# A 31-tap depthwise convolution traced tap by tap among the projections

## The chip, the cores and the metric

The kernel runs on one core of a Trainium2 chip. The metric is the device time of one launch in microseconds. The engines that matter here are TensorE (PE in the rows), VectorE (DVE), ScalarE (ACT) and GpSimd (POOL); the queue of SyncE (SP) issues most transfers. Each engine works through its own list of instructions in order and waits on semaphores for the others.

## The reference

One program computes a chain of layers on a sequence of 1024 tokens of width 1024. The change lies in the fourth stage of it, the even layer. Its core:

```python
hn = rmsnorm(x, norm_w)
proj = hn @ w_in
z_a, xbc, dt_raw, glu_v, glu_g, z_b = jnp.split(proj, idx, axis=-1)
xbc = silu(causal_dwconv(xbc, conv_w, conv_b))        # 4 taps
xs, bs, cs = jnp.split(xbc, ...)
dt = softplus(dt_raw + dt_bias)
y = ssd_chunked(xs, dt, a, bs, cs, d_skip)            # state-space scan
y_a = rmsnorm(y * silu(z_a))                          # per group
u = glu_v * sigmoid(glu_g)
u = causal_dwconv(u, dw_w, dw_b)                      # 31 taps, 1024 channels
u = silu(layernorm(u, ln_w, ln_b))
return x + concat([y_a, u * silu(z_b)]) @ w_out
```

The convolution of 31 taps works on each channel by itself: y[c, t] is the bias plus the sum over k of w[k, c] * u[c, t - 30 + k].

## The kernel before

`even` runs from about 1480 to 2125 us of the span. Matrix products are made in three matmuls each, from a high and a low half of both operands: `mm3` issues high x high (L264), high x low (L265) and low x high (L266) for every block of 128 rows. Weights come in by `load_w`: a transfer into `wr_t`, ScalarE makes the high half `wh_t` (L198), and VectorE (two thirds) and GpSimd (one third) make the low half `wl_t` (L203). The first L266 of a weight therefore waits for an L203 of VectorE.

The layer goes through four groups g = 0 to 3. A group holds, in the order in which it is traced:

- the gate z of the group (L1401), 192 matmuls of 256 columns, each bank read by VectorE (L1405);
- `glu(2g+1)`: 96 matmuls, then VectorE writes the channel block `u_t` (L1360) and hands it to `conv31`;
- `xbc` four times, for B, C, x0 and x1: 48 matmuls each, then on VectorE three short taps (L1380) and a product (L1383);
- in group 0 alone the running sums `cs` and their transposed copy `csT` (L1448), which the mask matmuls of every group read (L1488);
- transposes of B, x0 and x1 (L1437 for x0 and x1, after their L1383), mask matmuls (L1488, L1489), output gates (`gate_half`, 24 matmuls each) as fill;
- `glu(2g+2)` and its `u_t` (L1360);
- the scan, eight steps in a chain: VectorE's xd (L1508), TensorE's products (L1513, L1514, L1525), VectorE's L1516, L1528 (new state), L1517 and L1519, GpSimd's L1509, L1510, L1527 and L1518.

So there are eight channel blocks u0 to u7. `conv31(c, u)` makes one ScalarE instruction for tap 0 (L1338), 30 VectorE instructions over 128x1024 (L1340, called taps here), a GpSimd sum into `usum` (L1341) and a GpSimd transfer to DRAM. There are two `acc` buffers and two `u` buffers.

Nobody writes the order of an engine's list by hand. Instructions are traced with a rank (the order of tracing), and a planner puts on each engine the one of the best rank among those that it takes to be ready by its own model. `with self.later(LAG)` (L1336) adds 500 to the rank of all that a `conv31` traces, so that its taps go behind what is traced in the next 500 instructions and fill the gaps that these leave on VectorE.

Of the kernel before, what the change touches and what calls it, by code (L numbers as in the profile page):

```python
# [14 lines left out]
AF = mybir.ActivationFunctionType  # L15
ALU = mybir.AluOpType
# [3 lines left out]
P = 128  # L20
S = 1024
# [13 lines left out]
class Kern:  # L35
    def __init__(self, ctx, tc, a):
        self.tc, self.nc, self.a = tc, tc.nc, a
        self.n = 0
        self.reg = {}
        self.lo_dve = 0.66  # L40
        self.vcol = {}
        self.sb = self.cpool = ctx.enter_context(tc.tile_pool(name="const", bufs=1))
        self.dram = ctx.enter_context(tc.tile_pool(name="dram", bufs=1, space=bass.MemoryType.DRAM))

# [211 lines left out]
        return xh, xl  # L256


    def mm3(self, out, lhs, rhs, first, last):
        n = len(lhs)  # L260
        for i, ((lh, ll), (rh, rl)) in enumerate(zip(lhs, rhs)):
            st, en = first and i == 0, last and i == n - 1
            mm = self.nc.tensor.matmul
            mm(out, lh, rh, start=st, stop=False)  # L264
            mm(out, lh, rl, start=False, stop=False)  # L265
            mm(out, ll, rh, start=False, stop=en)  # L266


    def proj_T(self, ps, w, off, X):
# [1045 lines left out]
    def even(self, X, usum, rs, spill, zsp, ysp):  # L1315
        nc, a = self.nc, self.a
# [4 lines left out]
        cw31 = self.convw("a_dw_w_2", 31, 1024, 0.5)  # L1321
# [11 lines left out]
        b4 = lambda x: x.rearrange("p (e c) -> p e c", e=4)  # L1333

        def conv31(c, u):
            with self.later(LAG):  # L1336
                acc = self.slot("acc", [P, S])
                nc.scalar.activation(acc, u[:, 0:S], AF.Identity, scale=cw31(0, c), bias=self.col("a_dw_b_2", c))  # L1338
                for k in range(1, 31):
                    nc.vector.scalar_tensor_tensor(acc, u[:, k:k + S], cw31(k, c), acc, op0=ALU.mult, op1=ALU.add)  # L1340
                nc.gpsimd.tensor_tensor(usum, usum, acc, op=ALU.add)  # L1341
                nc.gpsimd.dma_start(out=spill[c], in_=acc)

        glw = {}

# [4 lines left out]
        def glu(c):  # L1350
            wg, wv = glw.pop(c)
            ps = self.psum("pb")
            self.proj_T(ps, wg, 0, X)
            th = self.slot("g", [P, S])
            nc.scalar.activation(th, ps, AF.Tanh, scale=0.5)
            ps = self.psum("pb")
            self.proj_T(ps, wv, 0, X)
            u = self.slot("u", [P, S + 30])
            nc.gpsimd.memset(u[:, 0:30], 0.0)
            nc.vector.scalar_tensor_tensor(u[:, 30:], th, 1.0, ps, op0=ALU.add, op1=ALU.mult)  # L1360
            conv31(c, u)
# [26 lines left out]
        for g in range(4):  # L1388
# [112 lines left out]
            for i in range(2):  # L1501
# [29 lines left out]
                for j in range(2):  # L1531
# [3 lines left out]
                    c = slice(i * 512, i * 512 + 512)  # L1535
                    yt = self.slot("zb", [P, 512])
                    nc.scalar.activation(yt, ps, AF.Copy, scale=gss[:, 2 * g + j:2 * g + j + 1])
                    nc.scalar.dma_start(out=ysp[2 * g + j, :, c], in_=yt)
            self.rsqrt(rstd, ss, 256 * 4, EPS, 8)

    def conf(self, hs, usum, rs, spill, zsp, ysp):
        nc, a = self.nc, self.a
# [525 lines left out]
```

## Time and profile before

| | us |
|---|---|
| median of 3 runs | 3085.46 |
| lowest and highest | 3083.87, 3091.32 |
| profiled execution | 3087.35 |
| its span | 3085.2 |
| outside the span | 2.15 |

| busy | TensorE | VectorE | ScalarE | GpSimd |
|---|---|---|---|---|
| whole span | 2910.8 (94%) | 2059.0 (67%) | 1192.9 (39%) | 1028.5 (33%) |
| 1480 to 2120 us | 608.18 of 640 | 557.59 | 193.93 | 225.38 |

The mean granted TensorE clock is 0.982. The 240 taps are 339.1 us of VectorE's time. A window row gives, for a stretch, the busy time of each engine and the number of its instructions; a timeline row gives an instruction's start, its duration, and in brackets how long its engine stood idle before it and which instruction let it go. Durations of neighbouring instructions overlap a little, so the distance of two starts is what one costs.

### The profile page before, as it was taken

Reading aid. Unit: us, or ns where it says so; the run is one execution under the profiler, and the core shown is the slowest. Engines: PE = TensorE matmul, PEld = TensorE weight load, DVE = VectorE, ACT = ScalarE, POOL = GpSimd, SP = SyncE. Lnnn points to the kernel's source line nnn. Section 1 sums busy time; section 2 is a strip of 40 time slices with the busy share of each in tenths; the row PEclk is TensorE's granted clock in tenths of the full one; section 3 lists DMA queues with packets and bytes.
Section 4 is the critical chain, followed back from the end, with each engine's and each line's share of the span. In section 5 each row is a group of like instructions: output and inputs, shape, how many; then the busy total and the mean of one; then the engine's idle time right before and its main releaser. Section 6 shows DMA issues by size and latency. Waiting matters only on the chain.

```text
span 3085.2 us, 39147 instructions
## 1 busy us (share of the span) xinstructions
PE 2910.8 (94%) x14462; PEld 2364.3 (77%) x14470; DVE 2059.0 (67%) x3296; ACT 1192.9 (39%) x2260; POOL 1028.5 (33%) x923
## 2 busy tenths in 40 slices
PE   8999899899899999999999999998999999999998
PEld 7777676677688887888877778786777888778776
DVE  4225789855765555444798979787697453178886
ACT  5422666634433333221332323223333332155654
POOL 2112611122765554231225251525331321121444
PEclk9999999899899999999999999999999999999999
DMA  3012100212122223431311212122522445244531
GB/s 118 30 49 66 35 1 8 69 41 76 42 96 88 80 86 137 139 109 45 93 52 45 62 48 61 46 65 69 212 69 96 127 144 181 83 134 144 169 92 65
DMA packets 179379, 259.93 MB, mean 84 GB/s; under 512 B 16605, under 2 KB 107253, under 8 KB 179189
## 3 DMA queue, kind: packets, MB, share of 16 engines
q1 hardware_dynamic: 157525, 218.64, 22.7%
q10 hardware_dynamic: 16768, 20.98, 2.1%
q0 software_dynamic: 4896, 17.83, 1.4%
q8 instruction: 114, 1.87, 0.3%
q14 instruction: 76, 0.62, 0.1%
HBM read 191.33 MB, written 66.06 MB: 83 GB/s over the span
## 4 chain that ended last, share of the span: by engine, by line
PE 64%; DVE 16%; issue 5%; POOL 4%; DMA 4%; ACT 3%; SPq 0%; POOLq 0%; DVEq 0%; ACTq 0%
PE pa_t L264 15%; PE pa_t L265 15%; PE pa_t L266 15%; DVE acc_t L1340 4%; PE pb_t L266 3%; PE pb_t L265 3%; PE pb_t L264 3%; PE pa_t L970 2%; PE pb_t L1065 1%; PE pa_t L1084 1%; DVE wl_t L203 1%; PE pb_t L1779 1%; PE pb_t L1780 1%; POOL wl_t L203 1%; DVE h_t L293 1%
## 5 line engine op out<-in xcount | busy, mean ns | idle before, releaser
L203 POOL TENSOR_TENSOR wl_t<-wr_t,wh_t 128x349 fp32r<-128x349 f32 (+3 forms) x199 | 240.0, 1212 | 975.0 <-ACT wh_t L198 919.3
L264 PE MATMUL pa_t<-wh_t,x_t 128*128 128x512 f32 (+3 forms) x1024 | 374.4, 366 | 2.7 <-ACT wh_t L198 0.6
L265 PE MATMUL pa_t<-wl_t,x_t 128*128 128x512 f32 (+3 forms) x1024 | 371.2, 363 | 0.5 <-DVE wl_t L203 0.5
L1340 DVE SCALAR_TENSOR_TENSOR acc_t<-u_t,c,acc_t 128x1024 f32<-128x1024 f32 x240 | 339.1, 1415 | 3.3 <-ACT acc_t L1338 0.4
L198 ACT CAST wh_t<-wr_t 128x1024 fp32r<-128x1024 f32 (+2 forms) x199 | 175.4, 890 | 352.4 <-PE pb_t L265 142.0
L291 DVE TENSOR_TENSOR h_t<-h_t,pa_t 128x512 f32<-128x512 f32 x256 | 173.1, 684 | 176.7 <-PE pa_t L266 174.9
L203 DVE TENSOR_TENSOR wl_t<-wr_t,wh_t 128x675 fp32r<-128x675 f32 (+2 forms) x173 | 166.8, 968 | 169.6 <-ACT wh_t L198 168.6
L264 PE MATMUL pb_t<-x_t,wh_t 128*128 128x512 f32 x616 | 247.9, 402 | 4.4 <-ACT wh_t L198 1.9
L266 PE MATMUL pb_t<-x_t,wl_t 128*128 128x512 f32 x616 | 244.9, 398 | 1.9 <-DVE wl_t L203 1.9
L265 PE MATMUL pb_t<-x_t,wh_t 128*128 128x512 f32 x584 | 233.7, 400 | 0.3 <-DVE x_t L394 0.3
L266 PE MATMUL pa_t<-wh_t,x_t 128*128 128x512 f32 (+3 forms) x640 | 221.4, 346 | 0.0
L264 PEld LDWEIGHTS pa_t<-wh_t,x_t 128*128 128x128 f32 x1024 | 192.3, 188 | 33.7 <-ACT wh_t L198 2.1
L265 PEld LDWEIGHTS pa_t<-wl_t,x_t 128*128 128x128 f32 x1024 | 192.5, 188 | 31.3 <-DVE wl_t L203 2.2
L266 PE MATMUL pa_t<-wh_t,xl_t 128*128 128x512 f32 x512 | 200.4, 392 | 3.0 <-POOL xl_t L1877 2.1
L332 ACT CAST wh_t<-wr_t 128x512 fp32r<-128x512 f32 x154 | 91.5, 620 | 238.7 <-POOL wr_t L340 127.6
L264 PE MATMUL pa_t<-x_t,wh_t 128*128 128x512 f32 x392 | 161.5, 412 | 2.6 <-DVE xt_t L391 1.3
L333 DVE TENSOR_TENSOR wl_t<-wr_t,wh_t 128x512 fp32r<-128x512 f32 x110 | 98.6, 916 | 90.9 <-ACT wh_t L332 90.9
L266 PE MATMUL pa_t<-x_t,wl_t 128*128 128x512 f32 x392 | 155.7, 397 | 0.0
L264 PEld LDWEIGHTS pb_t<-x_t,wh_t 128*128 128x128 f32 x616 | 117.0, 190 | 32.3 <-ACT wh_t L198 3.1
L265 PE MATMUL pa_t<-xt_t,wh_t 128*128 128x512 f32 x344 | 135.9, 395 | 4.9 <-DVE xt_t L372 4.3
L266 PEld LDWEIGHTS pb_t<-x_t,wl_t 128*128 128x128 f32 x616 | 116.7, 189 | 30.1 <-DVE wl_t L203 3.5
L209 ACT CAST pt_t<-pa_t 128x512 fp32r<-128x512 f32 (+2 forms) x240 | 104.8, 443 | 81.9 <-PE pa_t L970 46.0
(585 smaller groups left out, 7540.9 us busy)
## 6 DMA issues: line engine op xcount, KB each, us to landing
wr_t<-in_a_w_in SPq DMA_DIRECT2D x46, 512.0 KB
wr_t<-in_c_w_in SPq DMA_DIRECT2D x26, 512.0 KB
wr_t<-in_ffn_w_gate SPq DMA_DIRECT2D x22, 512.0 KB
wr_t<-in_ffn_w_up SPq DMA_DIRECT2D x22, 512.0 KB
wr_t<-in_ffn_w_down SPq DMA_DIRECT2D x44, 256.0 KB
yr_t<-yf SPq DMA_DIRECT2D x22, 512.0 KB
yf<-o_t SPq DMA_DIRECT2D x20, 512.0 KB
h_t<-in_x SPq DMA_DIRECT2D x16, 512.0 KB
```

The costliest lines, as they stand in the source:

```text
L198: nc.scalar.copy(hi, raw)
L203: e.tensor_tensor(*[x[:, c] for x in f], op=ALU.subtract)
L209: nc.scalar.copy(hi, src)
L264: mm(out, lh, rh, start=st, stop=False)
L265: mm(out, lh, rl, start=False, stop=False)
L266: mm(out, ll, rh, start=False, stop=en)
L291: self.nc.vector.tensor_tensor(h[t][:, c], h[t][:, c], ps, op=ALU.add)
L293: self.nc.vector.scalar_tensor_tensor(h[t][:, c], ps, rstd[:, t:t + 1], h[t][:, c], op0=ALU.mult, op1=ALU.add)
L332: nc.scalar.copy(hi, src)
L333: eng.tensor_tensor(lo, src, hi.bitcast(F32), op=ALU.subtract)
L970: self.nc.tensor.transpose(pt[:, i * 256 + q * P:i * 256 + (q + 1) * P], w[t0 + q][:, (b0 + i) * P:(b0 + i + 1) * P], self.ident)
L1340: nc.vector.scalar_tensor_tensor(acc, u[:, k:k + S], cw31(k, c), acc, op0=ALU.mult, op1=ALU.add)
```

## The change

`conv31` no longer traces its 30 taps at once with a lag. It puts them as 30 small calls into a list, `drip`. `mm3` calls `tick` after each three matmuls; each third call, so after nine matmuls, takes the next one off the list and traces it at that place, with the ordinary rank. What is left at the end of `even` is traced there. The `acc` buffer is taken with the first tap. Nothing computed is added or taken away; in numbers, VectorE, ScalarE, GpSimd, TensorE and SyncE issue the same instructions. The lists differ inside `even` alone.

```diff
--- before.py
+++ after.py
@@ -25,7 +25,6 @@
 EPS = 1e-6
 NEG = -1.0e30
 DFF = 2816
-LAG = 500
 AHEAD = 30
 ORDER = (6, 4, 2, 0)
 GATES_AT = 4
@@ -39,6 +38,7 @@
         self.reg = {}
         self.lo_dve = 0.66
         self.vcol = {}
+        self.drip, self.due = [], 0
         self.sb = self.cpool = ctx.enter_context(tc.tile_pool(name="const", bufs=1))
         self.dram = ctx.enter_context(tc.tile_pool(name="dram", bufs=1, space=bass.MemoryType.DRAM))
 
@@ -256,6 +256,13 @@
         return xh, xl
 
 
+    def tick(self):
+        self.due = min(self.due + 3, 9)
+        if self.drip and self.due == 9:
+            self.due = 0
+            self.drip.pop(0)()
+
+
     def mm3(self, out, lhs, rhs, first, last):
         n = len(lhs)
         for i, ((lh, ll), (rh, rl)) in enumerate(zip(lhs, rhs)):
@@ -264,6 +271,7 @@
             mm(out, lh, rh, start=st, stop=False)
             mm(out, lh, rl, start=False, stop=False)
             mm(out, ll, rh, start=False, stop=en)
+            self.tick()
 
 
     def proj_T(self, ps, w, off, X):
@@ -1333,13 +1341,20 @@
         b4 = lambda x: x.rearrange("p (e c) -> p e c", e=4)
 
         def conv31(c, u):
-            with self.later(LAG):
-                acc = self.slot("acc", [P, S])
-                nc.scalar.activation(acc, u[:, 0:S], AF.Identity, scale=cw31(0, c), bias=self.col("a_dw_b_2", c))
-                for k in range(1, 31):
-                    nc.vector.scalar_tensor_tensor(acc, u[:, k:k + S], cw31(k, c), acc, op0=ALU.mult, op1=ALU.add)
-                nc.gpsimd.tensor_tensor(usum, usum, acc, op=ALU.add)
-                nc.gpsimd.dma_start(out=spill[c], in_=acc)
+            acc = []
+
+            def begin():
+                acc.append(self.slot("acc", [P, S]))
+                nc.scalar.activation(acc[0], u[:, 0:S], AF.Identity, scale=cw31(0, c), bias=self.col("a_dw_b_2", c))
+                tap(1)
+
+            def tap(k):
+                nc.vector.scalar_tensor_tensor(acc[0], u[:, k:k + S], cw31(k, c), acc[0], op0=ALU.mult, op1=ALU.add)
+                if k == 30:
+                    nc.gpsimd.tensor_tensor(usum, usum, acc[0], op=ALU.add)
+                    nc.gpsimd.dma_start(out=spill[c], in_=acc[0])
+
+            self.drip += [begin] + [lambda k=k: tap(k) for k in range(2, 31)]
 
         glw = {}
 
@@ -1537,6 +1552,8 @@
                     nc.scalar.activation(yt, ps, AF.Copy, scale=gss[:, 2 * g + j:2 * g + j + 1])
                     nc.scalar.dma_start(out=ysp[2 * g + j, :, c], in_=yt)
             self.rsqrt(rstd, ss, 256 * 4, EPS, 8)
+        while self.drip:
+            self.drip.pop(0)()
 
     def conf(self, hs, usum, rs, spill, zsp, ysp):
         nc, a = self.nc, self.a
```

Lines of the changed file are shifted: L264 to L266 become L271 to L273, L1340 becomes L1352, L1360 L1375, L1380 L1395, L1383 L1398, L1448 L1463, L1449 L1464, L1508 L1523, L1513 L1528, L1514 L1529, L1516 L1531, L1517 L1532, L1519 L1534, L1525 L1540, L1528 L1543. L203 keeps its number.

The first place is TensorE's list in group 0 where `glu(1)` ends (`pb_t_12770` before, `pb_t_12765` after) and B begins (`pb_t_12887` and the weight `wl_t_12883` before, `pb_t_12853` and `wl_t_12849` after). Before:

```order
L264 MATMUL pb_t_12770<-x_t_12131,wh_t_12479 128x512
L265 MATMUL pb_t_12770<-x_t_12139,wh_t_12479 128x512
L266 MATMUL pb_t_12770<-x_t_12131,wl_t_12480 128x512
L264 MATMUL pb_t_12887<-x_t_12124,wh_t_12882 128x512
L265 MATMUL pb_t_12887<-x_t_12132,wh_t_12882 128x512
L266 MATMUL pb_t_12887<-x_t_12124,wl_t_12883 128x512
```

After (`pb_t_12942` is C's bank, and takes the place of `pb_t_12765`, from which VectorE reads for u1):

```order
L271 MATMUL pb_t_12765<-x_t_12131,wh_t_12445 128x512
L272 MATMUL pb_t_12765<-x_t_12139,wh_t_12445 128x512
L273 MATMUL pb_t_12765<-x_t_12131,wl_t_12446 128x512
L271 MATMUL pb_t_12853<-x_t_12124,wh_t_12848 128x512
L272 MATMUL pb_t_12853<-x_t_12132,wh_t_12848 128x512
L271 MATMUL pb_t_12942<-x_t_12124,wh_t_12937 128x512
L272 MATMUL pb_t_12942<-x_t_12132,wh_t_12937 128x512
L273 MATMUL pb_t_12853<-x_t_12124,wl_t_12849 128x512
```

B's low half is made on VectorE before the end of the z gates in the one, and behind u1 in the other; two matmuls of C, which need u1's bank, now stand ahead of B's first L273.

The second place is VectorE's list in group 0 from x0's product to x1's, with `csT` between them. Before:

```order
L1383 SCALAR_TENSOR_TENSOR g_t_13090<-g_t_13095,g_t_13090 128x1024
L1340 SCALAR_TENSOR_TENSOR acc_t_12822<-u_t_12819,c23_12271,acc_t_12822 128x1024
L1449 TENSOR_SCALAR cs_12857<-cs_12857 128x128
L1380 SCALAR_TENSOR_TENSOR g_t_13147<-pb_t_13098,c22_12265,g_t_13147 128x1023
L1448 TENSOR_TENSOR csT_13155<-pb_t_13156,csT_13155 16x1024
L1380 SCALAR_TENSOR_TENSOR g_t_13147<-pb_t_13098,c22_12265,g_t_13147 128x1022
L1340 SCALAR_TENSOR_TENSOR acc_t_12822<-u_t_12819,c23_12271,acc_t_12822 128x1024
L1380 SCALAR_TENSOR_TENSOR g_t_13147<-pb_t_13098,c22_12265,g_t_13147 128x1021
L1340 SCALAR_TENSOR_TENSOR acc_t_12822<-u_t_12819,c23_12271,acc_t_12822 128x1024
L203 TENSOR_TENSOR wl_t_13739<-wr_t_13736,wh_t_13738 128x675
L1383 SCALAR_TENSOR_TENSOR g_t_13147<-g_t_13152,g_t_13147 128x1024
```

After:

```order
L1398 SCALAR_TENSOR_TENSOR g_t_13074<-g_t_13079,g_t_13074 128x1024
L1352 SCALAR_TENSOR_TENSOR acc_t_12857<-u_t_12819,c23_12271,acc_t_12857 128x1024
L1464 TENSOR_SCALAR cs_12823<-cs_12823 128x128
L1352 SCALAR_TENSOR_TENSOR acc_t_12857<-u_t_12819,c23_12271,acc_t_12857 128x1024
L1395 SCALAR_TENSOR_TENSOR g_t_13137<-pb_t_13082,c22_12265,g_t_13137 128x1023
L1352 SCALAR_TENSOR_TENSOR acc_t_12857<-u_t_12819,c23_12271,acc_t_12857 128x1024
L1395 SCALAR_TENSOR_TENSOR g_t_13137<-pb_t_13082,c22_12265,g_t_13137 128x1022
L1463 TENSOR_TENSOR csT_13145<-pb_t_13146,csT_13145 16x1024
L1395 SCALAR_TENSOR_TENSOR g_t_13137<-pb_t_13082,c22_12265,g_t_13137 128x1021
L1352 SCALAR_TENSOR_TENSOR acc_t_12857<-u_t_12819,c23_12271,acc_t_12857 128x1024
L1398 SCALAR_TENSOR_TENSOR g_t_13137<-g_t_13142,g_t_13137 128x1024
```

`csT` has one tap and one L1380 ahead of it before, and three taps and two L1395 after; a weight's L203 that stood ahead of x1's product has gone behind it.

The third place is the scan of group 0. VectorE's list at its first steps before (`wl_t_13753` is the low half of the weight with which `glu(3)` begins, whose matmuls stand in TensorE's list between the steps of the scan):

```order
L1517 TENSOR_TENSOR y_t_13494<-y_t_13494,pa_t_13488 128x256
L1508 TENSOR_TENSOR xd_t_13529<-xs_t_13039,dt_12856 128x256
L203 TENSOR_TENSOR wl_t_13753<-wr_t_13750,wh_t_13752 128x675
L1519 TENSOR_TENSOR y_t_13494<-y_t_13494,sz_t_12484 128x256
L1516 TENSOR_TENSOR y_t_13517<-pa_t_13511,ecs_12858 128x256
L1528 TENSOR_TENSOR sst_13526<-sst_13526,pa_t_13524 128x256
L1517 TENSOR_TENSOR y_t_13517<-y_t_13517,pa_t_13511 128x256
L1508 TENSOR_TENSOR xd_t_13552<-xs_t_13039,dt_12856 128x256
L1340 SCALAR_TENSOR_TENSOR acc_t_13449<-u_t_13446,c23_12271,acc_t_13449 128x1024
```

The same weight is `wl_t_13724` after:

```order
L1523 TENSOR_TENSOR xd_t_13495<-xs_t_13018,dt_12822 128x256
L1352 SCALAR_TENSOR_TENSOR acc_t_13545<-u_t_13446,c23_12271,acc_t_13545 128x1024
L1534 TENSOR_TENSOR y_t_13460<-y_t_13460,sz_t_12450 128x256
...
L1534 TENSOR_TENSOR y_t_13506<-y_t_13506,sz_t_12450 128x256
L1531 TENSOR_TENSOR y_t_13529<-pa_t_13523,ecs_12824 128x256
L1543 TENSOR_TENSOR sst_13538<-sst_13538,pa_t_13536 128x256
L1532 TENSOR_TENSOR y_t_13529<-y_t_13529,pa_t_13523 128x256
L1523 TENSOR_TENSOR xd_t_13591<-xs_t_13019,dt_12822 128x256
L1523 TENSOR_TENSOR xd_t_13614<-xs_t_13019,dt_12822 128x256
L1534 TENSOR_TENSOR y_t_13529<-y_t_13529,sz_t_12450 128x256
L203 TENSOR_TENSOR wl_t_13724<-wr_t_13721,wh_t_13723 128x675
```

It has gone from the first step to behind the fourth one, and a tap has its place. TensorE's list of the steps two and three before:

```order
L1513 MATMUL pa_t<-xd_t,MT_t 128x64 x4
L1514 MATMUL pa_t<-sst,bc_t 128x256
L1525 MATMUL pa_t<-xd_t,bk_t 128x256
L266 MATMUL pb_t<-x_t,wl_t 128x512
L264 MATMUL pb_t<-x_t,wh_t 128x512
L265 MATMUL pb_t<-x_t,wh_t 128x512
L266 MATMUL pb_t<-x_t,wl_t 128x512
L264 MATMUL pb_t<-x_t,wh_t 128x512
L1513 MATMUL pa_t<-xd_t,MT_t 128x64 x4
L1514 MATMUL pa_t<-sst,bc_t 128x256
L1525 MATMUL pa_t<-xd_t,bk_t 128x256
L265 MATMUL pb_t<-x_t,wh_t 128x512
```

The steps two to four after:

```order
L1528 MATMUL pa_t<-xd_t,MT_t 128x64 x4
L1529 MATMUL pa_t<-sst,bc_t 128x256
L1540 MATMUL pa_t<-xd_t,bk_t 128x256
L1528 MATMUL pa_t<-xd_t,MT_t 128x64 x4
L1529 MATMUL pa_t<-sst,bc_t 128x256
L1540 MATMUL pa_t<-xd_t,bk_t 128x256
L1528 MATMUL pa_t<-xd_t,MT_t 128x64 x4
L1529 MATMUL pa_t<-sst,bc_t 128x256
L1540 MATMUL pa_t<-xd_t,bk_t 128x256
L271 MATMUL pa_t<-x_t,wh_t 128x512
```

The projection matmuls (L264 to L266) that stood between the steps are gone from there and stand after the scan. Over the whole scan 26 of them stand between steps before and 12 after, beside the 24 of the output gate in both (L271 in the last row is its first); in group 1 it is the same, and in group 2 they go from 20 to 9.

## Rows read from the trace of the kernel before

**Rows 1.** Windows of 40 us: length, busy time (instructions) by engine, PEclk, DMA share, GB/s.
```profile
1560.00:1600.00 40.00, 39.60 (x188) 32.08 (x186) 39.82 (x35) 11.90 (x14) 9.24 (x8) 1.00 0.13 40
...
1640.00:1680.00 40.00, 34.38 (x197) 27.79 (x196) 35.04 (x49) 10.73 (x28) 30.65 (x34) 1.00 0.15 46
...
sum 640.00, PE 608.18 PEld 504.41 DVE 557.59 ACT 193.93 POOL 225.38; mean PE 38.01 PEld 31.53 DVE 34.85 ACT 12.12 POOL 14.09
```

**Rows 2.** Waits of TensorE, 1480 to 2130 us: total, times, longest.
```profile
PE pa_t L1437 <- DVE g_t L1383: 9.9, 5, 3.1
```

**Rows 3.** Waits of VectorE, same stretch and columns.
```profile
DVE u_t L1360 <- PE pb_t L266: 49.5, 7, 10.6
```

**Rows 4.** The line of the taps: duration ns min/median/max, start us, forms.
```profile
L1340 DVE SCALAR_TENSOR_TENSOR acc_t<-u_t,c,acc_t x240: 1266/1284/3283, 1507.5 to 2120.5; 128x1024 f32<-128x1024 f32 x120
```

**Rows 5.** Timeline of VectorE, group 0: start, duration, line, op [idle before <-releaser].
```profile
1553.11 1.21 DVE L1360 SCALAR_TENSOR_TENSOR u_t<-g_t,pb_t 128x1024 f32<-128x1024 f32 x1
...
1598.59 0.85 DVE L203 TENSOR_TENSOR wl_t<-wr_t,wh_t 128x675 fp32r<-128x675 f32 x1
1599.36 1.22 DVE L1383 SCALAR_TENSOR_TENSOR g_t<-g_t 128x1024 f32<-128x1024 f32 x1
...
1603.81 1.22 DVE L1448 TENSOR_TENSOR csT<-pb_t,csT 16x1024 fp32r<-16x1024 f32 x1
...
1610.92 1.96 DVE L203 TENSOR_TENSOR wl_t<-wr_t,wh_t 128x675 fp32r<-128x675 f32 x1
1612.80 2.31 DVE L1383 SCALAR_TENSOR_TENSOR g_t<-g_t 128x1024 f32<-128x1024 f32 x1
```

**Rows 6.** Timeline of TensorE, group 0, same columns.
```profile
1551.06 0.40 PE L265 MATMUL pb_t<-x_t,wh_t 128*128 128x512 f32 x1
1551.30 0.40 PE L266 MATMUL pb_t<-x_t,wl_t 128*128 128x512 f32 x1
...
1600.64 1.09 PE L1437 MATMUL pa_t<-c,g_t 128*128 128x128 f32 x8 [0.77 <-DVE g_t L1383]
...
1605.17 0.93 PE L1488 MATMUL pa_t<-csT,c 128*128 128x512 f32 x2 [1.92 <-DVE csT L1448]
...
1608.26 0.63 PE L265 MATMUL pa_t<-x_t,wh_t 128*128 128x512 f32 x1
1608.69 0.63 PE L266 MATMUL pa_t<-x_t,wl_t 128*128 128x512 f32 x1
...
1615.25 1.06 PE L1437 MATMUL pa_t<-c,g_t 128*128 128x128 f32 x8 [0.83 <-DVE g_t L1383]
```

**Rows 7.** Timeline of VectorE, the scan of group 0.
```profile
1641.56 1.22 DVE L1360 SCALAR_TENSOR_TENSOR u_t<-g_t,pb_t 128x1024 f32<-128x1024 f32 x1 [8.97 <-PE pb_t L266]
...
1644.76 1.27 DVE L203 TENSOR_TENSOR wl_t<-wr_t,wh_t 128x675 fp32r<-128x675 f32 x1
...
1649.03 1.75 DVE L1340 SCALAR_TENSOR_TENSOR acc_t<-u_t,c,acc_t 128x1024 f32<-128x1024 f32 x1
...
1657.52 2.31 DVE L1340 SCALAR_TENSOR_TENSOR acc_t<-u_t,c,acc_t 128x1024 f32<-128x1024 f32 x1
1661.02 0.42 DVE L1519 TENSOR_TENSOR y_t<-y_t,sz_t 128x256 f32<-128x256 f32 x1 [1.19 <-POOL y_t L1518]
```

**Rows 8.** Timeline of TensorE, the scan of group 0.
```profile
1648.19 1.11 PE L1513 MATMUL pa_t<-xd_t,MT_t 128*128 128x64 f32 x8 [0.69 <-DVE sst L1528]
```

**Rows 9.** Timeline of VectorE, group 1.
```profile
1716.45 1.22 DVE L1360 SCALAR_TENSOR_TENSOR u_t<-g_t,pb_t 128x1024 f32<-128x1024 f32 x1 [1.54 <-PE pb_t L266]
...
1774.73 1.23 DVE L1383 SCALAR_TENSOR_TENSOR g_t<-g_t 128x1024 f32<-128x1024 f32 x1
```

**Rows 10.** Timeline of TensorE, group 1.
```profile
1776.10 0.63 PE L1437 MATMUL pa_t<-c,g_t 128*128 128x128 f32 x4 [3.07 <-DVE g_t L1383]
```

**Rows 11.** Windows of 4 us in group 0, columns as in Rows 1.
```profile
1604.00:1608.00 4.00, 2.83 (x8) 1.49 (x10) 3.97 (x4) 2.09 (x9) 0.88 (x1) 0.78 0.02 4
1608.00:1612.00 4.00, 4.00 (x16) 3.17 (x15) 4.00 (x3) 3.09 (x10) 4.00 (x3) 0.79 0.01 2
```

## The prediction

> **What bounds the kernel now.** I read the windows of the layer first. Over the 640 us from 1480 to 2120 TensorE is busy for 608.18, so some 32 us are to be had at most, and VectorE for 557.59; in the stretch of a group in which the projections of B, C and x run, both are full (39.60 and 39.82 of 40), and in the scan neither is (34.38 and 35.04) [rows 1]. So the bound changes: projections on both, the scan on its chain. Then TensorE's waits in the layer: the largest is for x0's and x1's product L1383 before the transposes L1437, 9.9 us in five waits [rows 2]. VectorE's waits come third: 49.5 us in seven waits at L1360 for the end of a glu [rows 3]. These two tell how a group goes: VectorE waits for TensorE at u, works through taps and short taps without a gap until x1, TensorE waits for x1, and VectorE is free again until the next u. The timeline of group 1 shows it: u3 starts when TensorE has ended (1.54 us idle before), x1 58.28 us later [rows 9], and TensorE waits 3.07 us for it [rows 10]. A tap takes 1.28 us (median of 240) [rows 4].
>
> **The change part by part.** No instruction goes or comes, so the sum is made of places where the order lets an engine wait longer or shorter.
>
> *Blocks from u to x1, groups 1 to 3: nothing by themselves.* Between u3, u5, u7 and the x1 after it stand 24 taps, 12 short taps, 3 products and 5 low halves L203 in either order. A gain by taps spread so that x1 comes sooner is not in the lists: a tap for every nine matmuls is 0.24 x 9 = 2.2 us of TensorE (two neighbouring starts [rows 6]), and the planner had them between the short taps already. So the 3.07 us stay, and whatever TensorE is late at u3 goes through to the end of the group.
>
> *Group 0, where B begins.* Between u0 and u1 VectorE now has 3 more taps and 3 fewer low halves. At 1.28 us [rows 4] and 1.27 us [rows 7] u1 doesn't move. But B's low half, made long before u1, now comes behind it. u1 starts at 1553.11 and takes 1.21 [rows 5], a low half 0.85, and TensorE is at its first L266 of B at 1551.30 [rows 6]: it stands until about 1555.2, less two matmuls of C, 3.4 us. All of that shows up only if VectorE is not the later one, and it is: from u1 to `csT` its list has one tap, one short tap and three low halves more, 1.28 + 1.27 + 3 x 0.85 [rows 5] = 5.1 us. The transposed copy then comes at about 1608.9 instead of 1603.81. TensorE waits for it already (1.92 us before L1488) [rows 6], so all 5.1 us arrive there; behind the mask matmuls and the 24 of the output gate TensorE had 0.83 us to wait for x1 [rows 6], which goes. x1 itself has only two low halves more ahead of it, and isn't the last. Sum: 5.1 - 0.83 = **+4.3 us**. The bounds: zero, if the scan behind u2 or a better overlap on GpSimd takes it up; and with low halves at the longest one, 1.96 us [rows 5], 5.1 + 3 x 1.11 - 0.83 = 7.6.
>
> *The scans of groups 0, 1 and 2.* Before, the low half of the next glu's weight is VectorE's first work beside the chain (1644.76, 1.27 us) [rows 7], and 26 projection matmuls fill TensorE's gaps between the steps. After, a tap has that place, the low half comes behind the fourth step, and 12 matmuls are left: 14 fewer in group 0 and in group 1, 11 fewer in group 2. They aren't lost but run behind the scan, in the stretch that ends in the next u, where TensorE is full and VectorE waits for it [rows 9]. That is 14 x 0.24 = 3.4, 3.4 and 2.6 us. Something comes back: in the scan TensorE waits for the state [rows 8] and VectorE once for GpSimd, 1.19 us before L1519 [rows 7]; in the new order of groups 0 and 1 the third step has no xd, GpSimd's multiplication for the masks stands ahead of the xd beside it, and this wait should go. In group 2 I see no such thing. So **+2.2, +2.2 and +2.6 us**. The bounds of each: -1.2 (the wait goes, the matmuls find other gaps, of which the scan stretch has 5.6 of 40 us [rows 1]) and +3.4. A tap in the place of a low half in the first step costs at most 1.75 or 2.31 instead of 1.27 [rows 7], beside GpSimd; the taps stood in the later steps at that price before, so I take nothing for it.
>
> *The end.* Six taps stand behind the last x1 in both orders, and the sum `usum` that the next layer's matmul waits for ends with them: nothing. SyncE's list is the same; the transfers to DRAM of a channel block wait for its last tap, and nobody waits for them before the next stage.
>
> The sum: 4.3 + 2.2 + 2.2 + 2.6 = 11.3 us, on the profiled execution's 3087.35 us 3098.65. That execution lies 1.89 us above the median of the runs, 3085.46, so the forecast on the median's scale is **3096.8 us**.
>
> **The rivals.** *Faster: x1 no longer late.* If in truth VectorE gets to x1 sooner, because a tap beside GpSimd costs 1.75 to 2.31 us [rows 7] and the new places avoid that, or because fewer than 24 taps stand ahead of x1 when it could start, TensorE's waits before L1437 go: 3085.46 - 9.9 = 3075.6. It decides from the point where each block from u to x1 is 3 us shorter, more than two taps. For it speaks that TensorE waits there five times; against it, the equal count. The Trainium skill (Perfetto Trace Analysis, Identifying the Most-Contended Engine) has a rule that points this way: where the most contended engine changes over time, interleaving the regimes may help. This case has such regimes, but its taps were spread over them before, so I see little left for the rule.
>
> *Same: the scans' matmuls cost nothing.* TensorE waits 3.07 us for x1 in group 1 [rows 10]. If VectorE doesn't really follow TensorE at u3, but its own 30 taps, whose end lies only 1.54 us before u3 [rows 9], then what TensorE is late is taken out of those waits: only group 0's 4.3 us stay, 3089.8. Against it: 1.54 us is idle time, so VectorE does wait; and 3.4 us exceed the 3.07.
>
> *Slower: the clock.* In group 0, behind the wait for `csT`, the granted clock is 0.78 and 0.79 in two windows of 4 us [rows 11], between the levels of 1.2 and 2.4 GHz, and two neighbouring matmuls start 0.43 us apart instead of 0.24 [rows 6]. That is 4 x 0.22 + 4 x 0.21 = 1.7 us. With steps of the scan that have no projection matmul in them, and with the stand before B, the same can happen at four more places: +6.8 us, 3103.6. It decides where TensorE's stands get as long as those ahead of 1604; the matmuls of the scan itself keep it at work, which speaks against it. The Trainium skill (TensorE: Matmul & The Clock Gate, HAM oscillation — how this bites in real kernels) tells of kernels whose small stands between groups of matmuls send the clock up and down; the scans of before have small stands and full clock (1.00) [rows 1], so here the trace doesn't bear it out yet.
>
> **How the numbers follow.** The forecast gets 0.5, same 0.25, the clock 0.13, faster 0.12. A change of 0.3%, 9.3 us, is about what can be told from none here: the limits are 3076.2 and 3094.7. The forecast's own range is 3090 to 3101, with one part in five below 3094.7; so slower has 0.40 + 0.13 = 0.53, same 0.25 + 0.10 = 0.35, faster 0.12. The bounds of the terms, 0 to 7.6 and three times -1.2 to 3.4 (2.6 in group 2), give -3.6 to +17.0, or 3081.9 to 3102.5; the clock takes the upper end to 3106. Range 3082 to 3106; the faster case lies outside.
>
> **What would show it.** Right: the wait before L1488 for `csT` at 6 to 7 us; a stand of about 3.4 us at B's first L273 near 1552; hardly any idle time before L1437 at x1 in group 0, and about 3 us in groups 1 and 2 as before; u3's idle time at L1375 grown by some 2 us; the stretch from u2 to u3 longer by 2 us. Wrong: waits before L1437 gone; the distance from u3 to x1 other than 58.3 us; windows of low clock in the scans; a layer shorter than before; or a difference behind 2125 us, where the lists are the same.

## The result and the profile after

The changed kernel takes 3105.64 us (median of four runs, 3104.50 to 3112.60), the kernel before 3087.64 us beside it (four runs, 3083.87 to 3091.32). The ratio is 1.0072, 95% interval [1.0057, 1.0086]: slower by some 18 to 26 us on 3085. The direction was forecast, the size was not: 11.3 us were, and 3085.46 x 1.0072 = 3107.7 lies above the range (the median itself lies just inside its end of 3106, beside runs of before that were 2.2 us above 3085.46). The profiled execution took 3104.50 us (span 3102.7), 17.2 more than that of before.

Where the time went is read best from the starts of the eight u (the line L1360, now L1375) and of x1's product (L1383, now L1398), since both engines pass through them. The distances, each the difference of two starts on VectorE's timeline:

| us | before | after | difference |
|---|---|---|---|
| u0 to x1, group 0 | 107.91 | 111.37 | +3.5 |
| x1 to u2, group 0 | 28.76 | 40.29 | +11.5 |
| u2 to u3 (scan of group 0) | 74.89 | 78.33 | +3.4 |
| u3 to x1, group 1 | 58.28 | 56.96 | -1.3 |
| x1 to u4, group 1 | 27.59 | 26.91 | -0.7 |
| u4 to u5 (scan of group 1) | 74.91 | 78.09 | +3.2 |
| u5 to u6, group 2 | 85.88 | 85.57 | -0.3 |
| u6 to u7 (scan of group 2) | 88.64 | 89.27 | +0.6 |
| u7 to the end of the span | 1033.45 | 1032.49 | -1.0 |

So 15.0 of the 19.0 us between u0 and the end lie between u0 and u2, by VectorE's starts most of them behind x1 of group 0, where the forecast had let VectorE be free. The timeline of VectorE after, from `csT` to the read of the output gate's bank (start, duration, line, op; the answer to [rows 5]):

```profile
1611.08 1.21 DVE L1463 TENSOR_TENSOR csT<-pb_t,csT 16x1024 fp32r<-16x1024 f32 x1
...
1614.79 1.23 DVE L1398 SCALAR_TENSOR_TENSOR g_t<-g_t 128x1024 f32<-128x1024 f32 x1
1615.94 2.30 DVE L1352 SCALAR_TENSOR_TENSOR acc_t<-u_t,c,acc_t 128x1024 f32<-128x1024 f32 x1
1618.16 1.95 DVE L203 TENSOR_TENSOR wl_t<-wr_t,wh_t 128x675 fp32r<-128x675 f32 x1
1620.04 8.28 DVE L1352 SCALAR_TENSOR_TENSOR acc_t<-u_t,c,acc_t 128x1024 f32<-128x1024 f32 x4
1628.24 0.67 DVE L1386 SCALAR_TENSOR_TENSOR zb_t<-zb_t,pa_t 128x512 f32<-128x512 f32 x1
```

Behind x1 stand a tap, a low half and four taps, and only then L1386, which reads the bank of the first output gate. It starts 13.45 us behind x1. In the kernel before, the same read (L1371, start 1616.22 us) stands 3.42 us behind x1 [rows 5], with one tap ahead of it. The four taps take 8.28 us, 2.07 each instead of the usual 1.28, most of it beside GpSimd's multiplications:

```profile
1615.87 7.61 POOL L1509 TENSOR_TENSOR MT_t<-MT_t,cb_t 128x512 f32<-128x512 f32 x4 [9.67 <-ACT MT_t L1508]
1623.59 1.45 POOL L1524 TENSOR_TENSOR xd_t<-xs_t,dtds 128x256 f32<-128x256 f32 x1
1625.97 1.27 POOL L1509 TENSOR_TENSOR MT_t<-MT_t,cb_t 128x512 f32<-128x512 f32 x1 [0.93 <-ACT MT_t L1508]
```

TensorE in the same stretch and at B (the answer to [rows 6]):

```profile
1552.21 0.60 PE L271 MATMUL pb_t<-x_t,wh_t 128*128 128x512 f32 x1 [2.26 <-DVE u_t L1375]
...
1555.72 0.79 PE L273 MATMUL pb_t<-x_t,wl_t 128*128 128x512 f32 x1 [2.49 <-DVE wl_t L203]
...
1612.44 1.64 PE L1503 MATMUL pa_t<-csT,c 128*128 128x512 f32 x2 [4.55 <-DVE csT L1463]
...
1628.97 0.79 PE L1503 MATMUL pa_t<-csT,c 128*128 128x512 f32 x1 [4.11 <-DVE zb_t L1386]
```

It stands idle four times: 2.26 and 2.49 us at B (for u1's bank, then for B's low half), 4.55 us for `csT`, 4.11 us for the gate's bank, since the third mask matmul behind x1 needs that bank (a bank is a piece of the memory in which TensorE adds up its products; the kernel writes one anew only when the product before has been read out of it). The last two waits were 1.92 us and nothing in the kernel before. TensorE's waits of the layer, 1480 to 2150 us (total, times, longest; the answer to [rows 2]):

```profile
PE pa_t L1452 <- DVE g_t L1398: 9.4, 3, 3.9
PE pa_t L1528 <- DVE sst L1543: 8.2, 5, 2.8
PE pa_t L1503 <- DVE csT L1463: 4.5, 1, 4.5
PE pa_t L1503 <- DVE zb_t L1386: 4.1, 1, 4.1
...
PE pb_t L273 <- DVE wl_t L203: 2.5, 1, 2.5
PE pb_t L271 <- DVE u_t L1375: 2.3, 1, 2.3
```

Of the waits for x0 and x1, the two of group 0 (0.77 and 0.83 us [rows 6]) are gone, as the prediction had it for x1; in the other groups they are 9.4 us in all, and were 8.3. And behind each stand the granted clock is down. Six windows of 4 us of the kernel after (columns as in [rows 1]; the last numbers are PEclk, DMA share and GB/s):

```profile
1552.00:1556.00 4.00, 1.30 (x3) 0.57 (x4) 4.00 (x5) 1.24 (x1) 2.98 (x4) 0.56 0.31 131
1612.00:1616.00 4.00, 3.56 (x8) 1.68 (x9) 3.97 (x5) 2.30 (x7) 0.13 (x1) 0.50 0.00 0
1616.00:1620.00 4.00, 4.00 (x16) 3.23 (x16) 4.00 (x3) 2.89 (x12) 4.00 (x3) 0.83 0.00 0
1628.00:1632.00 4.00, 3.03 (x7) 1.93 (x8) 4.00 (x6) 0.00 (x0) 1.41 (x1) 0.50 0.17 66
1632.00:1636.00 4.00, 4.00 (x14) 3.14 (x14) 0.40 (x1) 0.00 (x0) 4.00 (x4) 0.70 0.00 0
1664.00:1668.00 4.00, 3.49 (x13) 2.59 (x12) 3.85 (x6) 1.37 (x6) 3.31 (x4) 0.50 0.01 2
```

0.50 is the level of 1.2 GHz. The last window lies in the scan of group 0, behind a new stand of 2.80 us:

```profile
1662.06 1.97 PE L1528 MATMUL pa_t<-xd_t,MT_t 128*128 128x64 f32 x8 [2.80 <-DVE sst L1543]
```

In the same scan of before the window from 1640 to 1680 has 1.00 [rows 1].

### The profile page after: what moved, and what is told of

The parts are those of the page before. It is cut to its first block, busy times and chain, and to the rows that moved or that the text cites. A ratio compares the mean times of both kernels' runs of the same rounds, so it can differ in the third digit from the quotient of the medians.

```text
span 3102.7 us, 39151 instructions
## 1 busy us (share of the span) xinstructions
PE 2923.5 (94%) x14462; PEld 2374.5 (77%) x14470; DVE 2064.5 (67%) x3296; ACT 1193.6 (38%) x2260; POOL 1024.3 (33%) x923
## 4 chain that ended last, share of the span: by engine, by line
PE 62%; DVE 18%; issue 6%; POOL 4%; ACT 3%; DMA 3%; SPq 0%; POOLq 0%; ACTq 0%; DVEq 0%
PE pa_t L271 15%; PE pa_t L272 15%; PE pa_t L273 15%; DVE acc_t L1352 5%; PE pb_t L273 2%; PE pb_t L272 2%; PE pb_t L271 2%; PE pa_t L978 2%; DVE wl_t L203 1%; PE pb_t L1073 1%; PE pa_t L1092 1%; PE pb_t L1796 1%; PE pb_t L1797 1%; DVE g_t L1395 1%; DVE bc_t L1395 1%
## 5 line engine op out<-in xcount | busy, mean ns | idle before, releaser
L203 POOL TENSOR_TENSOR wl_t<-wr_t,wh_t 128x349 fp32r<-128x349 f32 (+3 forms) x199 | 241.0, 1218 | 987.5 <-ACT wh_t L198 952.9
L271 PE MATMUL pa_t<-wh_t,x_t 128*128 128x512 f32 (+3 forms) x1024 | 374.5, 366 | 2.9 <-ACT wh_t L198 0.9
L1352 DVE SCALAR_TENSOR_TENSOR acc_t<-u_t,c,acc_t 128x1024 f32<-128x1024 f32 x240 | 336.6, 1402 | 2.6 <-ACT acc_t L1348 0.4
L203 DVE TENSOR_TENSOR wl_t<-wr_t,wh_t 128x675 fp32r<-128x675 f32 (+2 forms) x173 | 168.4, 977 | 182.5 <-ACT wh_t L198 181.5
L271 PE MATMUL pb_t<-x_t,wh_t 128*128 128x512 f32 x616 | 247.9, 402 | 6.0 <-DVE u_t L1375 2.3
L273 PE MATMUL pb_t<-x_t,wl_t 128*128 128x512 f32 x616 | 246.5, 400 | 3.7 <-DVE wl_t L203 3.7
L273 PE MATMUL pa_t<-wh_t,x_t 128*128 128x512 f32 (+3 forms) x640 | 221.2, 346 | 0.0
L271 PEld LDWEIGHTS pa_t<-wh_t,x_t 128*128 128x128 f32 x1024 | 192.3, 188 | 34.3 <-ACT wh_t L198 2.5
L273 PE MATMUL pa_t<-wh_t,xl_t 128*128 128x512 f32 x512 | 200.0, 391 | 3.0 <-POOL xl_t L1894 2.1
L271 PE MATMUL pa_t<-x_t,wh_t 128*128 128x512 f32 x392 | 162.9, 416 | 1.7 <-DVE xt_t L399 0.8
L273 PE MATMUL pa_t<-x_t,wl_t 128*128 128x512 f32 x392 | 155.8, 397 | 0.0
L271 PEld LDWEIGHTS pb_t<-x_t,wh_t 128*128 128x128 f32 x616 | 117.5, 191 | 34.3 <-DVE u_t L1375 2.7
L273 PEld LDWEIGHTS pb_t<-x_t,wl_t 128*128 128x128 f32 x616 | 117.2, 190 | 32.1 <-DVE wl_t L203 5.2
```

The costliest lines, as they stand in the source:

```text
L203: e.tensor_tensor(*[x[:, c] for x in f], op=ALU.subtract)
L1352: nc.vector.scalar_tensor_tensor(acc[0], u[:, k:k + S], cw31(k, c), acc[0], op0=ALU.mult, op1=ALU.add)
```

## The experiments

Theory 1 is that the head of group 0 costs the time, by TensorE's stands at B, at `csT` and at the gate's bank, with the clock that falls behind them. Theory 2 is the forecast: 4.3 us in the head, the rest in the scans. Later runs split theory 1: 1a, the read of the gate's bank is on the path; 1b, it isn't, and B and `csT` make the 15 us. Distances are from one profiled execution each (the same head gave 151.66 and 152.07 us in two kernels); ratios are against runs of the kernel before on the same chip.

**Only the blocks of the head tap by tap.** u0 and u1 as in the changed kernel, the others as before:

```diff
         def conv31(c, u):
+            if c >= 2:
+                with self.later(500):
+                    ...
+                return
             acc = []
```

> Only the channel blocks u0 and u1 go tap by tap; u2 to u7 are traced as a block with a lag of 500, as before. VectorE's list of group 0 up to u2 is then that of the changed kernel, and the scans have the projection matmuls between their steps that they had before (26, 26, 20). Theory 1 (the head of group 0: TensorE stands at B, at csT and at the output gate's bank, each time with a lower granted clock behind it; 15.0 us from u0 to u2): 12 to 16 us above the kernel before, u0 to u2 150 to 152 us long. Theory 2 (the forecast: 4.3 us in the head, the rest in the scans): 3 to 6 us above before.

3096.72 us against 3085.46, ratio 1.0035 [1.0022, 1.0047]. u0 to u2 is 152.07 us; u2 to u3 and u4 to u5 are 74.90 and 74.89, as before. From u0 to the end of the span it is 13.0 us longer than before. This is what theory 1 expected, except that by the ratio it is 10.8 us, a little under the 12 to 16.

**Only the rest tap by tap.** The same edit with `c < 2`.

> The other half: u0 and u1 are traced as a block with the lag, u2 to u7 go tap by tap. The head of group 0 is that of before, the scans have 10 to 14 fewer projection matmuls between their steps. Theory 1: 2 to 5 us above the kernel before. Theory 2: 7 us above before, and up to 13 with a low clock in three scans.

3087.91 us, ratio 1.0009 [1.0000, 1.0019]. u0 to u2 is 137.50 us, the scans are 78.38, 78.22 and 89.74; u0 to the end is 5.6 us longer than before. From u0 on the two halves add up: 13.0 + 5.6 = 18.6 us, and the whole change has 19.0. By the ratios they don't: 10.8 and 2.8 us make 13.6, and the whole change is 22.2, with intervals that barely meet. The split is one of profiled executions, and good to a few us. Theory 2 falls by the head of the first half, though not its sum for the scans.

**`csT` first.** The instructions that make `csT` are traced 300 ranks earlier.

```diff
             if g == 0:
-                csT = ...
+                with self.later(-300):
+                    csT = ...
```

> The changed kernel, with the three instructions of csT traced 300 ranks earlier. In the list csT stands right behind x0's product, and the output gate's L1386 two instructions behind x1's instead of seven. The stand at B stays. Theory 1: the waits of 4.55 and 4.11 us and the low clock behind them go, 12 to 14 us less than the changed kernel, 4 to 6 above before. If the stands count but the clock costs nothing: 7 to 9 us less. Theory 2: 4 us less at most.

3092.08 us, ratio 1.0020 [1.0010, 1.0029], so 6 us above before and some 16 below the changed kernel by the two ratios; u0 to u2 is 138.95 us, 12.7 less than in the changed kernel. VectorE's list moved in both places, as its timeline shows:

```profile
1602.46 1.21 DVE L1464 TENSOR_TENSOR csT<-pb_t,csT 16x1024 fp32r<-16x1024 f32 x1
...
1613.91 2.23 DVE L1398 SCALAR_TENSOR_TENSOR g_t<-g_t 128x1024 f32<-128x1024 f32 x1
1616.06 2.29 DVE L1352 SCALAR_TENSOR_TENSOR acc_t<-u_t,c,acc_t 128x1024 f32<-128x1024 f32 x1
1618.28 0.67 DVE L1386 SCALAR_TENSOR_TENSOR zb_t<-zb_t,pa_t 128x512 f32<-128x512 f32 x1
```

`csT` follows x0, and L1386 has one tap ahead of it. The gate's matmuls stand behind `csT` in TensorE's list, so the planner's model presumably has the gate's read ready that much sooner. So this run doesn't tell the two waits apart. TensorE now waits at x1 (1.59 us) as it did before.

**`csT` first, and TensorE kept busy at B.** 20 matmuls more ahead of B's first.

```diff
             ps = self.psum("pb")
+            for _ in range(20 if ch == 8 else 0):
+                mm(ps[:, 0:512], xh[0][:, 0:P], xh[1][:, 0:512], start=True, stop=True)
```

> As the kernel with csT first, and 20 matmuls of 512 columns more ahead of B's first one, into B's bank, whose result is overwritten: TensorE works through the 4.8 us in which it stands there (1549.8 to 1555.7 in the changed kernel). If the stand brings the clock down: the windows from 1552 to 1560 show 1.00 instead of 0.56 and 0.59, and B's first matmuls start 0.24 us apart instead of 0.43; u0 to u2 is 1.5 to 3.4 us shorter than with csT first alone, in spite of 20 matmuls more. If the clock falls for another reason, or VectorE sets the pace there: the same clock, or the same time within 1 us.

The clock came out as expected. The window behind the stand with `csT` first alone:

```profile
1552.00:1556.00 4.00, 1.90 (x5) 1.51 (x6) 4.00 (x5) 0.00 (x0) 1.36 (x3) 0.50 0.50 160
```

and with the 20 matmuls:

```profile
1552.00:1556.00 4.00, 2.79 (x13) 1.95 (x12) 4.00 (x6) 0.00 (x0) 0.97 (x2) 1.00 0.60 190
```

TensorE still waits there, 1.21 us for the low half, but doesn't stand long, and its first matmuls of B start 0.23 us apart instead of 0.43. The time did not follow: u0 to u2 is 141.05 us, 2.1 longer (ratio to before 1.0043 [1.0030, 1.0057]; the profiled execution, 3089.24 us, is the fastest of five with a median of 3097.49). From u1 to x1 it is 1.2 us longer (65.77 against 64.59), but in another list: it has eight low halves there and the other seven. With `csT` first alone VectorE waits twice in that stretch, 1.14 us for TensorE's sums (L1434) and 0.86 us for a high half of ScalarE; with the 20 matmuls neither wait is left, and the eighth low half takes 1.86 us. From x1 to u2 it is 0.9 us longer: 92 matmuls of the glu stand behind x1's transposes instead of 88, at 0.23 us each. So no gain by the clock is to be seen, but since VectorE's list changed too, the run doesn't show whether the stand at B lies on the path.

**The gate's read late in the kernel before.** 24 short instructions on VectorE behind x1's product:

```diff
             nc.vector.scalar_tensor_tensor(o, th, 1.0, o, op0=ALU.add, op1=ALU.mult)
+            for i in range(24 if ch == 1 else 0):
+                q = th[:, i % 4 * 256:i % 4 * 256 + 256]
+                nc.vector.scalar_tensor_tensor(q, q, 1.0, q, op0=ALU.mult, op1=ALU.add)
```

> The kernel before, with 24 short VectorE instructions (128x256, on a tile that is no longer read) behind x1's product of group 0, so ahead of the output gate's L1371; nothing else is moved. Theory 1a (in the head the read of the gate's bank sets the end, since the mask matmuls' next bank waits for it): TensorE waits 6 to 9 us at L1488 for L1371, with a lower clock behind it, and u0 to u2 is 144 to 148 us instead of 136.67. Theory 1b (the stands at B and csT make the 15 us; VectorE is free behind x1, as the forecast took it): u0 to u2 within 2 us of before.

Theory 1b's figure: 3086.11 us, ratio 1.0001 [0.9988, 1.0014], u0 to u2 137.14. The read did come late, but TensorE never waited for it. VectorE's rows, and TensorE's in the half in question:

```profile
1616.90 10.73 DVE L1386 SCALAR_TENSOR_TENSOR g_t<-g_t 128x256 f32<-128x256 f32 x24
1627.55 0.67 DVE L1371 SCALAR_TENSOR_TENSOR zb_t<-zb_t,pa_t 128x512 f32<-128x512 f32 x1
```

```profile
1616.62 0.47 PE L1491 MATMUL pa_t<-csT,c 128*128 128x512 f32 x1
...
1616.97 0.58 PE L1491 MATMUL pa_t<-csT,c 128*128 128x512 f32 x1
...
1617.59 0.50 PE L1491 MATMUL pa_t<-csT,c 128*128 128x512 f32 x1
...
1618.64 0.50 PE L1491 MATMUL pa_t<-csT,c 128*128 128x512 f32 x1
```

All four mask matmuls (L1491) run without a wait. TensorE's list shows why: the planner, which had the added instructions in its model, gave the third of them another bank. In the changed kernel the third mask matmul of this half waits for VectorE (in the kernel before, the second does):

```
L1503 pa_t_13320<-csT_13145,c10_97 [waits DVE_49]
```

and here for ScalarE:

```
L1491 pa_t_13352<-csT_13179,c10_97 [waits Activation_49]
```

So this run did not make the wait that it was to make. A late read costs only where TensorE's next work uses that bank. u2 to u3 is 77.99 us, 3.1 more than before; from u0 to the end of the span nothing of it is left (1579.14 against 1580.31 us).

**A lag of 300.** `LAG = 300` in the kernel before.

> The kernel before with a lag of 300 for the taps instead of 500. In VectorE's list B's low half has gone behind u1 and one tap, csT has one tap more ahead of it, the gate's L1371 stands two instructions behind x1's product as before, the scans are as before. Theory 1a: a stand of about 5 us at B with a low clock, but u0 to u2 only 2 to 5 us longer than the 136.67 of before. Theory 1b: 9 to 12 us longer.

u0 to u2 is 140.90 us, 4.2 longer, inside theory 1a's 2 to 5. TensorE stands 0.94 and 1.38 us at B and 3.23 us for `csT`, and 0.30 for the gate's bank. The ratio is 1.0013 [0.9999, 1.0027]; the profiled execution, 3082.45 us, is the fastest of ten with a median of 3090.35. At B some 5 us of standing were expected and 2.3 came, so the run says little about a stand of the size that the change has there.

**A tap for every six matmuls.** `tick` counts to 6.

> The changed kernel with a tap for every six matmuls instead of nine. In groups 1 to 3, where there is no csT, the gate's L1386 now stands behind five taps (three in group 3), two low halves and two xd after x1's product, instead of next to it. Theory 1a: TensorE stands for it in each of these groups, and x1 to the next u is 35 to 40 us instead of 26.9 and 29.0; 3120 to 3140 us in all. Theory 1b: 27 to 30 us there.

A miss: 3102.79 us, ratio 1.0043 [1.0023, 1.0064], less than with one in nine. x1 to u4 and to u6 are 29.52 and 28.93 us, theory 1b's figure and not 35 to 40. No mask matmul stands for L1386 in any group, though it is late in all of them: in groups 1 to 3 of this list none of them depends on VectorE, and in group 0 the one that does comes when the bank has just been freed. So this run, like the one with the late read, doesn't test theory 1a: the lateness of a read in the list is no forecast of a wait. In group 0, u0 to u2 is 145.82 us, with a wait of another kind, a projection's for the bank that a short tap reads:

```profile
PE pb_t L271 <- DVE g_t L1395: 5.3, 1, 5.3
```

**`csT` first and the glu weights first.** Beside the edit for `csT`:

```diff
         def glu_w(c):
             if c < 8:
-                glw[c] = [...]
+                with self.later(-300 if c % 2 else 0):
+                    glw[c] = [...]
```

> The changed kernel with csT first, and besides the weights of glu 1, 3, 5 and 7 traced 300 ranks earlier: their low half stands ahead of the scan, and 30 projection matmuls stand between the steps in groups 0 and 1, 23 in group 2 (12, 12 and 4 in the changed kernel, 26, 26 and 16 before). If the missing matmuls make the scans longer (3.4, 3.3 and 1.1 us with csT first): u2 to u3, u4 to u5 and u6 to u7 come to 74 to 75, 74 to 75 and 87 to 89 us, and the kernel is 6 to 8 us faster than with csT first alone, within 2 us of before. If not: 78, 78 and 89 us as there.

The scans are 74.36, 74.36 and 87.59 us instead of 78.08, 78.21 and 89.78: 9.8 us back, 3.7 and 3.9 in groups 0 and 1. 3082.75 us, ratio 0.9991 [0.9979, 1.0003], so by the two ratios 9 us faster than with `csT` first alone, and not to be told from the kernel before. It is the low half's place, then, and with it the matmuls in the gaps and the clock, that made the scans longer. How much of it is the clock wasn't measured by itself. (Group 2 has 20 such matmuls in the list before and 9 in the changed one; the 16 and 4 of the expectation are another count.)

**The gate's bank freed by ScalarE.** In the changed kernel, for the first gate alone:

```diff
+            if c == 0 and hf == 0:
+                for q in (slice(0, 256), slice(256, 512)):
+                    zc = self.small(256, tag="y", bufs=4)
+                    nc.scalar.copy(zc, ps[:, q])
+                    nc.vector.scalar_tensor_tensor(z[:, q], z[:, q], 1.0, zc, op0=ALU.add, op1=ALU.mult)
+            else:
                 nc.vector.scalar_tensor_tensor(z, z, 1.0, ps, op0=ALU.add, op1=ALU.mult)
```

> The changed kernel, in which the first output gate of group 0 leaves its bank by two ScalarE copies, and VectorE's L1386 (two halves, at the same place in its list, behind five taps and a low half) reads the copies. TensorE's next bank then no longer waits for VectorE. VectorE's list is otherwise the same, csT and B come as late as in the changed kernel. Theory 1a (the three stands of TensorE follow one another on the path, the gate's bank among them): the wait of 4.11 us and the low clock behind it go, u0 to u2 is 144 to 147 us instead of 151.66. Theory 1b (the gate's bank only hides what csT and B cost; another wait takes its place): 149 to 152 us.

u0 to u2 is 144.79 us: 6.9 less than in the changed kernel, as theory 1a had it. VectorE's read is as late as there, and TensorE no longer cares; the stand for `csT` is unchanged:

```profile
1610.59 1.23 DVE L1404 SCALAR_TENSOR_TENSOR g_t<-g_t 128x1024 f32<-128x1024 f32 x1
...
1615.82 8.39 DVE L1352 SCALAR_TENSOR_TENSOR acc_t<-u_t,c,acc_t 128x1024 f32<-128x1024 f32 x4
1624.14 0.75 DVE L1390 SCALAR_TENSOR_TENSOR zb_t<-zb_t,y_t 128x256 f32<-128x256 f32 x2
```

```profile
1608.23 1.64 PE L1509 MATMUL pa_t<-csT,c 128*128 128x512 f32 x2 [4.54 <-DVE csT L1469]
```

The ratio to before is 1.0037 [1.0023, 1.0051], about half of the change's 1.0072.

**The bank freed, and TensorE kept busy for `csT`.** 18 matmuls ahead of the first mask matmul, as at B.

> As the kernel with the gate's bank freed, with 18 matmuls of 512 columns more ahead of the first L1503 of group 0, into its own bank, whose result is overwritten: TensorE works through the 4.55 us in which it stands for csT. VectorE's list is the same. If the low clock behind the stand lies on the path: the windows behind csT show 1.00 (0.50 and 0.83 in the changed kernel), and u0 to u2 is 2 to 4 us shorter than with the bank freed alone, with more work. If VectorE sets the pace there: the clock is up, and u0 to u2 the same within 1 us.

u0 to u2 is 143.79 us, 1.0 shorter, ratio 1.0038 [1.0024, 1.0051]. The window behind `csT`, first with the bank freed alone, then with the 18 matmuls:

```profile
1608.00:1612.00 4.00, 3.77 (x8) 1.88 (x10) 3.97 (x5) 2.51 (x8) 0.34 (x1) 0.50 0.01 4
```

```profile
1612.00:1616.00 4.00, 3.65 (x15) 2.07 (x15) 3.94 (x4) 0.74 (x2) 0.00 (x0) 1.00 0.00 0
```

The clock is up again, and u0 to u2 gained 1.0 us, not 2 to 4. But `csT` itself came 0.8 us later after u0 here (108.22 against 107.45). From the first mask matmul to u2, over the same matmuls (the 18 lie ahead of it), it is 34.31 us instead of 35.98 with the bank freed alone:

```profile
1614.27 0.96 PE L1511 MATMUL pa_t<-csT,c 128*128 128x512 f32 x2 [0.35 <-DVE csT L1469]
```

So the low clock lies on the path there, with 1.7 us.

**The kernel before with `csT` and the glu weights first.** The two edits on the kernel before.

> The kernel before (the block with its lag), with csT first and the glu weights first, as in the kernel with both. The wait of 1.92 us for csT and the clock of 0.78 behind it should go: u0 to u2 133 to 136 us instead of 136.67, the scans 74.4, 74.4 and 87.6 instead of 74.9, 74.9 and 88.6. 2 to 5 us faster than before. If the waits for x1 take it up: the same within 1 us.

3083.89 us, ratio 0.9998 [0.9987, 1.0009]: the same. u0 to u2 is 135.23 us, 1.4 less, and the scans of groups 0 and 1 are 74.40 and 74.31, but that of group 2 is 89.28 us, where 87.6 were expected and 88.64 were before. The wait for x1 in group 0 is 2.38 us now instead of 0.83 [rows 6], and the transposes of cs wait 1.8 us for x0: the stand moved on to x0 and x1. The gain of 2 to 5 us did not come.

**One in twelve, with both first.** `tick` counts to 12, and the two edits.

> The changed kernel with a tap for every twelve matmuls instead of nine, csT first and the glu weights first. B's low half is made ahead of u1 in this list, the gate's L1386 stands two instructions behind x1's product, and 30, 30 and 23 projection matmuls fill the scans. If the three places and the scans are all that the change costs: none of the stands of group 0, u0 to u2 134 to 138 us, the scans as with both put first, 1 to 5 us faster than the kernel before. If the spreading itself costs something: slower than before.

3084.58 us, ratio 0.9996 [0.9987, 1.0005]. u0 to u2 is 135.32 us, the scans 74.32, 74.31 and 89.28 (87.59 with both put first at one in nine, so group 2 is a miss), and the gain of 1 to 5 us did not come. No stand at B or `csT` is left, only 2.28 us before the transposes of cs, which wait for x0, and 2.38 us for x1. So in this list, which is close to that of before, taps traced one by one cost nothing; nor do they gain anything. None of the versions is faster than the kernel before by more than the measurement can tell.

## Why the prediction was wrong

- **Direction and place: right in kind.** The change makes nothing faster, and the loss lies in `even`. Blocks from u to x1 were put at nothing: they came out at -1.3, -1.7 and +0.9 us, for a reason that wasn't tried.
- **The scans: the sum right, its parts not.** 2.2 + 2.2 + 2.6 = 7.0 us were forecast; 3.4 + 3.2 + 0.6 = 7.2 were measured, and the run with the weights first shows that the place of the low half is the cause. That the sums agree is luck: the give-back of 1.2 us in groups 0 and 1 didn't come (VectorE still waits 1.20 us for GpSimd there), and in group 2 the loss was 2.0 us smaller than forecast. Since other stretches became shorter, the kernel is only 4.0 us longer behind u2, where 7.0 were forecast.
- **The head of group 0: the step that failed.** "5.1 - 0.83 = +4.3 us" stood for 15.0, and it went wrong in two places. The first is the path. Its sentence "behind the mask matmuls and the 24 of the output gate TensorE had 0.83 us to wait for x1 [rows 6], which goes" ends the path at x1. It goes on: the third mask matmul behind x1 needs the bank that VectorE frees by L1386, and five taps and a low half stood ahead of that in the list. The forecast had taken what VectorE does between x1 and u2 to be free, since it waits 8.97 us at u2 [rows 7]. From the transposes of x1 to u2 both kernels issue the same number of matmuls, in 26.31 us before [rows 6] and in 32.84 now, from this row on:

```profile
1622.24 1.03 PE L1452 MATMUL pa_t<-c,g_t 128*128 128x128 f32 x8
```

That is 6.5 us for what was put at nothing: 4.11 of standing, and 2.4 of slower matmuls behind it. The second place is the term of 5.1 us: `csT` came 9.4 us later after u1 (60.14 against 50.70 us), and 8.7 after u0. The tap, the short tap and the three low halves were counted rightly. But seven low halves took 8.0 us where four had taken 3.6, a short instruction for dt (L1319, 1.55 us) had moved behind u1, and VectorE, which did not wait in this stretch before, waited twice:

```profile
1570.03 0.29 DVE L1435 COPY cs<-pa_t 128x128 f32<-128x128 f32 x1 [1.32 <-PE pa_t L1434]
...
1581.94 0.86 DVE L203 TENSOR_TENSOR wl_t<-wr_t,wh_t 128x675 fp32r<-128x675 f32 x1 [0.87 <-ACT wh_t L198]
```

So the transposes of x1 start 8.5 us later after u0 (118.82 against 110.36), where 4.3 were forecast, and 8.5 + 6.5 = 15.0. The wait for `csT` was 4.55 us and not the 6 to 7 of the prediction, because TensorE itself came to it 6.1 us later after u0 than before. The runs give a like split: 6.9 us for the gate's bank (freed by ScalarE), a further 5.8 when `csT` comes first as well (144.79 to 138.95 us, in a list where the gate's read is early too), and 2.3 that are left with B's stand still there (138.95 to 136.67).
- **B: sized a little low; its place on the path stays open.** 3.4 us were forecast; the two waits are 4.75. Keeping TensorE busy there saved nothing in the time, but it took away the two waits of VectorE between u1 and x1, in a list with one low half more there. What B costs by itself no run shows.
- **The clock: a rival with 0.13, and it was there.** Each stand of 2 us or more in group 0 was followed by windows of 0.50 to 0.83. The Trainium skill (TensorE: Matmul & The Clock Gate, A second HAM failure mode: psum-queue depth-cycling, the section behind the one that the prediction names) tells of a kernel in which short idle times between groups of matmuls send the clock down and up again, and here the trace agrees, with 0.50 in three windows of 4 us. Its price at `csT` was 1.7 us on the path, which is what the rival asked for each place, and behind the gate's bank some 2.4 us by the rows above, an estimate. The prediction read full clock in the scans from one window of group 0. Over the three whole scans the granted clock was 1.00, 0.98 and 0.96 before, is 0.93, 0.96 and 0.94 in the changed kernel, and 1.00, 0.98 and 0.96 again with the weights first; what that is worth was not tried apart. The range's upper end of 3106 has no working: the prediction's own bound and this rival's price give 3102.5 + 6.8 = 3109.3.
- **The two other rivals.** The waits for x1 did not go (9.4 of 9.9 us left), so nothing came out faster. And the scans' matmuls were not free. The Trainium skill's sentence on interleaving that the prediction weighs stands in Perfetto Trace Analysis, Optimization Strategy; no run here shows a gain by it.

## What to carry to other kernels

An engine with idle time is not free at every place in its list: look for the reads that empty an accumulation bank, and for what stands ahead of them, before an order is called harmless behind the last product. When a planner sets the order, rank decides only among what its model takes to be ready; with `csT` moved forward, the read of the gate moved too, and 12.7 of the head's 15.0 us came back. And a late read costs nothing where the waiting engine's next work uses another bank (the run with the late read), nor is anything gained by a stand that goes when another wait takes its place (`csT` first in the kernel before): which bank comes next in the list has to be looked up.

## What was not expected of the hardware

Four taps of 128x1024 on VectorE took 8.28 us beside GpSimd's work, 2.07 each, against a median of 1.28 [rows 4]; before had single ones of 1.75 and 2.31 [rows 7]. 18 to 20 useless matmuls in a stand brought the granted clock from 0.50 back to 1.00 in the window behind it, and at `csT` the added work cost no time (143.79 against 144.79 us).
